# Two passes of a down-projection piece held back and issued behind the next block's first gate/up product

## The chip, the cores and the metric

The kernel runs on one core of a Trainium2 chip. The metric is the device time of one execution in microseconds (us). TensorE (PE in the profile) multiplies, with its weight loads shown as PEld; VectorE is DVE, ScalarE is ACT, GpSimd is POOL, and SyncE (SP) issues most DMAs.

## The reference

Two layers of a decoder trunk over 512 tokens of width 1024. Each layer has a mixer of three kinds of heads, a gated MLP, and a per-layer embedding. The part in which the change lies is the MLP and the projection of the embedding:

```python
def conv_gated_mlp(h, w_gate, w_up, conv_w, conv_b, w_down):
    g = h @ w_gate                      # 512 x 1024 by 1024 x 4096
    gp = jnp.pad(g, ((0, 0), (CONV_WIDTH - 1, 0), (0, 0)))
    conv = conv_b + gp[:, 0:S] * conv_w[0]
    for j in range(1, CONV_WIDTH):
        conv = conv + gp[:, j:j + S] * conv_w[j]
    act = jax.nn.gelu(conv, approximate=True) * (h @ w_up)
    return act @ w_down                 # 512 x 4096 by 4096 x 1024
...
h = rmsnorm(x, ffn_pre_g[i])
x = x + rmsnorm(conv_gated_mlp(h, ...), ffn_post_g[i])
gate = jax.nn.sigmoid(rmsnorm(x, ple_pre_g[i]) @ w_ple_gate[i])
e = p[i] @ w_ple_proj[i]                # 512 x 256 by 256 x 1024
x = x + rmsnorm(e * gate, ple_post_g[i])
```

Everything is float32.

## The kernel before

**Products in three passes.** A float32 product is made of two rounded halves of each operand, high and low (`split`: ACT writes the high half, DVE the low half). `mm3` issues three passes for each 128 rows of contraction: high by high, high by low, low by high. A pass is one MATMUL with its own weight load of 128 by 128.

**The MLP in 32 blocks.** Block `b` makes 128 of the 4096 gate and up columns, for all 512 tokens. `gate_up(b)` does this with seven products in place of eight (a Strassen-like scheme): the tokens are two halves of 256, the contraction two halves of 512. Each product is 4 x 3 = 12 passes of 256 columns. Its names, in the order in which they are recorded, with the names that the profile shows:

| product | written to | operands in the profile |
|---|---|---|
| b11 | `be`, bank `beta` | `beta<-hb,wg` |
| b21 | `al`, bank `ag` | `ag<-hb,wg` |
| h6 | `be` | `beta<-hh,wsa` |
| d | `ga`, bank `ag` | `ag<-hd,wsa` |
| h7 | `be` | `beta<-hh,wsb` |
| b22 | `ga` | `ag<-hb,wsb` |
| h4 | `be` | `beta<-hh,wu` |

`be` keeps accumulating over four products. Between them ACT copies it out (`gs<-beta` behind b11 and behind h6), DVE reads it (`us<-beta,us` behind h7), and the next product into `be` waits for that read. So h6 waits for ACT, h7 for ACT, and h4 for DVE's `us`. In the same way d waits for DVE's `gs<-ag,gs`, and b22 for ACT's `us<-ag`.

**The down projection in pieces.** Every four blocks give 512 columns of the activation (`act`, two blocks to a tile). They are multiplied with their part of `w_down` one group of four later: eight pieces `down(q, c, u)`, one for each 128 tokens `c` and each half of the output. A piece is 4 x 3 = 12 passes of 512 columns into a PSUM bank `dn` (`dn<-thl,act`), and DVE adds the bank to an accumulator (`facc<-dn,facc`; ACT copies it for the first group). Blocks 4 to 31 of a layer issue such pieces behind their seven products, mostly two each, so 24 passes; the last group's eight pieces stand behind the blocks. `embed` makes the product of the embedding ahead of block 0 (`eps<-ehl,pT`: 8 pieces of 6 passes, each copied out by ACT and stored by a DMA from SP's queue).

**What sets the order.** The code records every operation in a `Plan`. `Plan.issue` then walks the recorded operations with estimated costs (`cost`), takes on each engine the earliest recorded one that is ready, and so fills PE's expected waits with passes recorded later. What comes out is issued through one line (L396), so the profile's rows are told apart by tiles. The built program differs a little from the plan's order, because the layer underneath also moves a few PE instructions; the rows shown below are those of the built program. Large tiles come from two sets of slots (`SETS`), and `pick` chooses the set.

Of the kernel before, what the change touches and what calls it, by code (L numbers as in the profile page):

```python
# [32 lines left out]
ALU = mybir.AluOpType  # L33
# [5 lines left out]
NCH = 4  # L39
# [10 lines left out]
class Plan:  # L50
# [18 lines left out]
    def __init__(self):  # L69
        self.ops = []  # L70
        self.table = {}
        self.tiles = {}
        self.real = {}
        self.kind = {}
        self.place = {}
        self.scratch = bacc.Bacc("TRN2", target_bir_lowering=False, num_devices=1)

    def pool(self, pool, psum=False):

# [62 lines left out]
    def record(self, engine, fn, method, args, kw):  # L142
        i = len(self.ops)
        outs, ins = [], []
        first = True
        for k, v in [(None, v) for v in args] + list(kw.items()):
            if not isinstance(v, bass.AP):
                continue
            is_out = k in ("out", "accum_out") or (k is None and first)
            if k is None:  # L150
                first = False
            (outs if is_out else ins).append(v)
        deps, used = set(), []
        for aps, write in ((ins, False), (outs, True)):
            for ap in aps:
                name = ap.tensor.name
                if name not in self.tiles or self.tiles[name][0] == "junk":
                    continue
                t = self.tiles[name]
                used.append(name)  # L160
                r = (0, P, [(0, 512)]) if t[3] else self.region(ap)
                for j, w, q in t[2]:
                    if (write or w) and j != i and j not in deps and self.overlap(r, q):
                        deps.add(j)
                t[2].append((i, write, r))
        if engine == "PE":
            t = self.tiles[outs[0].tensor.name]
            if len(t) > 6:
                deps.add(t[6])
            t[6:] = [i]  # L170
        self.ops.append((engine, fn, args, kw, deps, used, self.cost(engine, method, outs, ins, args, kw)))

    def cost(self, engine, method, outs, ins, args, kw):

        def size(ap):
            n = 1
            for d in ap.shape[1:]:
                n *= d
            return n

        if "dma" in method:
            return (820 if engine == "POOL" else 525) if outs[0].shape[0] > 2 else 700, 4.0 * size(outs[0]) * outs[0].shape[0]
        n = size(ins[0] if method == "tensor_reduce" else outs[0])
        psum = any(self.tiles[v.tensor.name][3] for v in ins + outs)
        scalars = [kw.get(k) for k in ("scalar", "scalar1", "scalar2", "bias", "scale")]
        pointers = sum(isinstance(v, bass.AP) for v in scalars)
        if engine == "PE":
            if method == "transpose":
                return 108, 0, n
            dt, rows = kw["lhsT"].dtype, kw["lhsT"].shape[0] / P  # L190
            if dt == F32R:
                return 0.4416 * n + 6, 0, n * rows
            half = 0.5 if kw["lhsT"].shape[0] == 64 or kw["lhsT"].shape[-1] == 64 else 1
            return half * max(222, n * 4 / 2.4 + 4) if dt == F32 else max(56, n / 2.4), 0, (2 if dt == F32 else 1) * n * rows
        if engine == "ACT":
            func = ([v for v in args if isinstance(v, AF)] + [None])[0]
            self.table[len(self.ops)] = func if func in self.TABLES else None
            pointers += method == "mul" and isinstance(args[2], bass.AP)
            return (50 if psum else 97) + n / 1.196 + 93 * pointers + 93 * ("accum_out" in kw), 0
        if engine == "POOL":  # L200
            if n > 64:
                return 155 + n * (2.09 if method == "tensor_tensor" else 0.86), 0
            if kw.get("op") == ALU.pow:
                return 300 + 165 * n, 0
            return 160 if pointers == 0 else 200 + 64 * pointers, 0
        rate = 0.96
        if method == "reciprocal":
            rate /= 8
        elif method in ("tensor_copy", "tensor_scalar") and not psum:
            rate *= 2  # L210
        return 68 + 62 * bool(pointers) + n / rate, 0

    def issue(self):
        ops = self.ops
        n = len(ops)
# [10 lines left out]
        first, last, slots, live = {}, {}, {}, {}  # L226
# [18 lines left out]
        done = [False] * n  # L245
        front = 0
# [23 lines left out]
        def pick(t):  # L270

            if self.kind[t] is not None:
                c, s = self.kind[t], first[t]
                return c if unused[c] and (s <= front or inside[c][front:s].max() < self.SETS[c]) else None
            room = [(self.SETS[c] - inside[c][front:last[t] + 1].max(), c) for c in self.SETS if unused[c]]
            spare, c = max(room, default=(0, None))
            return c if spare > 0 else None

        def take(i, now):
            o = ops[i]  # L280
# [70 lines left out]
        while len(order) < n:  # L351
            progress = False
            for e in names:
                while waiting[e] and waiting[e][0][0] <= now:
                    _, pr, i = heapq.heappop(waiting[e])
                    heapq.heappush(ready[e], (pr, i))
                if ready[e] and free[e] <= now:
                    _, i = heapq.heappop(ready[e])
# [108 lines left out]
def body(ctx, tc, a, out):  # L467
# [259 lines left out]
    def mm3(ps, lhs, rhs, first, last, skip=False):  # L727
        for i, (h, r) in enumerate(((0, 0), (0, 1), (1, 0))):
            T.matmul(ps, lhsT=lhs(h), rhs=rhs(r), start=first and i == 0, stop=last and i == 2, skip_group_check=skip)
# [317 lines left out]
    def ffn(l, hs, emb, x, new, g, nxt):  # L1047
# [11 lines left out]
        def product(ps, w, n, first, last):  # L1059
            for k in range(4):  # L1060
                ks = slice(k * P, k * P + P)
                mm3(ps, lambda i: w[i][:, ks], lambda i: h[n][:, i, k, :], first and k == 0, last and k == 3, True)

        def gate_up(b):
            raw = b8("graw", (2048,))
            load(raw, a["w_gu"][l, b].rearrange("p s n -> p (s n)"))
            u2, g1, g2, u1 = (raw[:, i * 512:i * 512 + 512] for i in range(4))
# [19 lines left out]
            def part(t, i):  # L1087
                return [t[:, j, i * 512:i * 512 + 512] for j in range(2)]
            product(be, part(wg, 0), "b11", True, False)
            A.copy(gs[:, t1], be)  # L1090
            product(al, part(wg, 1), "b21", True, True)
            V.tensor_tensor(out=gs[:, t1], in0=al, in1=gs[:, t1], op=ALU.add)
# [19 lines left out]
            t = acts[b // 2]  # L1112
            split(t[:, 0, b % 2, :], t[:, 1, b % 2, :], cv)

        def down(q, c, u):

            ps = bank("dn")
            ts = slice(c * P, c * P + P)
            for j in range(4):
                t = acts[2 * q + j // 2]  # L1120
                mm3(ps, lambda i: t[:, i, j % 2, ts], lambda i: u(i, j), j == 0, j == 3)
            return ps

        def wd(q, hf):
            return tm_units(a["w_dn"][l, q, hf], 512, 4)

        embed(l, *emb)
        for b in range(32):
            gate_up(b)
            q, i = divmod(b, 4)  # L1130
            if not q:
                continue
            i0, i1 = ((0, 2, 4, 6, 8) if q < 7 else (0, 1, 3, 5, 8))[i:i + 2]
            for hf, c in [divmod(j, 4) for j in range(i0, i1)]:
                if c == 0:
                    u = wd(q - 1, hf)
                ps = down(q - 1, c, u)
                if q == 1 and hf == 0 and c % 2 == 0:
                    facc.append(b8("facc", (2, D)))
                fr = facc[c // 2][:, c % 2, hf * 512:hf * 512 + 512]  # L1140
                if q == 1:
                    A.copy(fr, ps)
                else:
                    V.tensor_tensor(out=fr, in0=ps, in1=fr, op=ALU.add)

        us = [wd(7, hf) for hf in range(2)]
        for c in range(NCH):
# [1 line left out]
        for c in range(NCH):  # L1149
            fr = facc[c // 2][:, c % 2, :]  # L1150
            parts = []
            for hf in range(2):
                ps = down(7, c, us[hf])
                cs = slice(hf * 512, hf * 512 + 512)
                V.tensor_tensor(out=fr[:, cs], in0=ps, in1=fr[:, cs], op=ALU.add)
                parts.append(post_part(fr[:, cs], g[:, 0, cs], fr[:, cs]))
            post_chunk(x[c], parts, fr, stored=new[:, c, :])
            nxt(c, x[c])
# [25 lines left out]
    def embed(l, pT, us):  # L1184

        e = [b8("e", (2, D)) for _ in range(2)]
        for hf, u in enumerate(us):
            cs = slice(hf * 512, hf * 512 + 512)
            for c in range(NCH):
                ps = bank("eps")  # L1190
                ts = slice(c * P, c * P + P)
                for k in range(2):
                    mm3(ps, lambda i: pT[:, i, k, ts], lambda i: u[:, i, k, :], k == 0, k == 1)
                A.copy(e[c // 2][:, c % 2, cs], ps)
                SY.dma_start(out=ed[l][:, c, cs], in_=e[c // 2][:, c % 2, cs])

    ov = out[0].rearrange("(c p) d -> p c d", p=P)

# [92 lines left out]
```

## Time and profile before

| | us |
|---|---|
| time before, median of 3 runs (1637.95 to 1641.28) | 1638.48 |
| the profiled execution's own time | 1644.15 |
| its span, first to last instruction | 1642.3 |
| PE busy in the span | 1598.1 (97%) |
| DVE, ACT busy in the span | 1240.5, 840.4 |

The profiled execution is 5.7 us longer than the median, 1.9 us of its own time lie outside its span. A row of the timeline gives the start of a run of equal instructions and its stretch; matmuls are pipelined, so what a run takes is the difference between its start and that of the next run. In the groups and the windows, busy time is summed over overlapping instructions.

### The profile page before, as it was taken

To read this page: it belongs to the slowest core of one execution; us is meant where nothing else is said; L and a number is where in the kernel's file an instruction comes from. 1 tells how busy PE (TensorE), PEld (TensorE's weight loads), DVE (VectorE), ACT (ScalarE), POOL (GpSimd) and SP (SyncE) were. 2 spreads that over 40 slices of the span, in tenths; PEclk is the share of its full clock that TensorE was granted. 3 is DMA by queue.
4 is the path that set the end of the run, shared out by engine and by line. 5 is a ranking of instruction groups with operands and counts; after the bars stand their busy time and mean duration, and the time that the engine had idled before them with its cause. 6 is when DMAs were issued, how large, how long until landed. Compare 5 with 4: busy or idle time off the path is not lost.

```text
span 1642.3 us, 25129 instructions
## 1 busy us (share of the span) xinstructions
PE 1598.1 (97%) x10034; PEld 1411.3 (86%) x10034; DVE 1240.5 (76%) x1949; ACT 840.4 (51%) x1378; POOL 90.5 (6%) x157
## 2 busy tenths in 40 slices
PE   5999999999999999999999999989999999999998
PEld 4887687999999999998878776879999999999987
DVE  6456758987888888786764568599788788788784
ACT  5435626765554554554562346276555555555453
POOL 1100012000000000001220000110000000000022
PEclk9999999999999999999999999999999999999999
DMA  7313316323324323236552133172334233233441
GB/s 281 104 38 129 105 64 216 118 79 128 103 78 129 100 81 129 97 103 256 193 172 82 65 103 116 53 253 82 104 103 129 78 104 129 77 103 129 173 161 65
DMA packets 63422, 197.48 MB, mean 120 GB/s; under 512 B 7349, under 2 KB 15165, under 8 KB 63305
## 3 DMA queue, kind: packets, MB, share of 16 engines
q1 hardware_dynamic: 63016, 195.28, 35.1%
q8 instruction: 79, 1.29, 0.3%
q10 hardware_dynamic: 288, 0.59, 0.1%
q14 instruction: 39, 0.31, 0.1%
HBM read 178.52 MB, written 17.33 MB: 119 GB/s over the span
## 4 chain that ended last, share of the span: by engine, by line
PE 71%; DVE 5%; ACT 3%; DMA 3%; issue 1%; POOL 1%; SPq 0%; POOLq 0%; DVEq 0%; ACTq 0%
PE beta L396 20%; PE dn L396 20%; PE ag L396 15%; PE ps L396 7%; PE fps L396 2%; PE rps L396 2%; PE wo L396 1%; DVE x L396 1%; PE gps L396 1%; DMA traw<-in_w_dn_dram 1%; ACT junk L396 1%; DMA e<-e 1%; PE hps L396 1%; PE ops L396 0%; ACT thl L396 0%
## 5 line engine op out<-in xcount | busy, mean ns | idle before, releaser
L396 PE MATMUL dn<-thl,act 128*128 128x512 f32 x1536 | 368.0, 390 | 0.0
L396 PEld LDWEIGHTS dn<-thl,act 128*128 128x128 f32 x1536 | 282.7, 188 | 54.0
L396 PE MATMUL ps<-thl,hT 128*128 128x512 f32 (+3 forms) x984 | 206.3, 369 | 0.0
L396 PEld LDWEIGHTS ps<-thl,hT 128*128 128x128 f32 x984 | 178.2, 190 | 21.9
L396 DVE TENSOR_TENSOR thl<-traw,thl 128x1024 fp32r<-128x1024 f32 (+2 forms) x120 | 141.3, 1187 | 37.0 <-ACT thl L396 36.2
L396 ACT CAST thl<-traw 128x1024 fp32r<-128x1024 f32 (+2 forms) x120 | 121.0, 1019 | 44.9 <-PE fps L396 11.1
L396 PE MATMUL beta<-hb,wg 128*128 128x256 f32 x768 | 105.8, 283 | 5.6 <-DVE wg L396 5.6
L396 PEld LDWEIGHTS beta<-hb,wg 128*128 128x128 f32 x768 | 101.5, 191 | 10.3 <-DVE wg L396 6.0
L396 ACT COPY gs<-beta 128x256 f32<-128x256 f32 x128 | 47.6, 372 | 112.1 <-PE beta L396 112.0
L396 PE MATMUL ag<-hb,wg 128*128 128x256 f32 x768 | 103.2, 283 | 0.0
L396 PE MATMUL beta<-hh,wsa 128*128 128x256 f32 x768 | 101.8, 282 | 1.2 <-ACT gs L396 0.9
L396 PE MATMUL beta<-hh,wsb 128*128 128x256 f32 x768 | 101.7, 281 | 0.2
L396 PE MATMUL beta<-hh,wu 128*128 128x256 f32 x768 | 101.7, 282 | 0.2
L396 DVE TENSOR_TENSOR wsa<-ws,wsa 128x1024 fp32r<-128x1024 f32 x64 | 78.2, 1221 | 31.2 <-ACT wsa L396 25.7
L396 PEld LDWEIGHTS beta<-hh,wu 128*128 128x128 f32 x768 | 93.9, 188 | 9.0 <-DVE us L396 7.6
L396 PE MATMUL ag<-hd,wsa 128*128 128x256 f32 x768 | 100.8, 281 | 0.7 <-DVE gs L396 0.7
L396 PE MATMUL ag<-hb,wsb 128*128 128x256 f32 x768 | 100.7, 280 | 0.0
L396 PEld LDWEIGHTS beta<-hh,wsa 128*128 128x128 f32 x768 | 95.4, 190 | 2.1 <-ACT gs L396 1.4
L396 PEld LDWEIGHTS ag<-hb,wg 128*128 128x128 f32 x768 | 96.6, 191 | 0.0
L396 DVE SCALAR_TENSOR_TENSOR cv<-gs,cw,cv 128x511 f32<-128x511 f32 (+1 forms) x128 | 95.5, 746 | 1.4 <-ACT cv L396 0.3
L396 PEld LDWEIGHTS beta<-hh,wsb 128*128 128x128 f32 x768 | 94.6, 189 | 1.5 <-ACT gs L396 1.3
L396 PEld LDWEIGHTS ag<-hd,wsa 128*128 128x128 f32 x768 | 94.7, 189 | 1.3 <-DVE gs L396 1.1
(194 smaller groups left out, 2711.8 us busy)
## 6 DMA issues: line engine op xcount, KB each, us to landing
graw<-in_w_gu_dram SPq DMA_DIRECT2D x128, 512.0 KB
traw<-in_w_dn_dram SPq DMA_DIRECT2D x64, 512.0 KB
x<-x SPq DMA_DIRECT2D x40, 512.0 KB
fraw<-in_w_fm_dram SPq DMA_DIRECT2D x30, 512.0 KB
traw<-in_w_wo_dram SPq DMA_DIRECT2D x16, 512.0 KB
traw<-in_w_pg_dram SPq DMA_DIRECT2D x16, 512.0 KB
traw<-in_w_uv_dram SPq DMA_DIRECT2D x8, 512.0 KB
e<-e SPq DMA_DIRECT2D x16, 256.0 KB
```

Of the source, the lines that this page charges most:

```text
L396: o[1](*[self.map(v) for v in o[2]], **{k: self.map(v) for k, v in o[3].items()})
```

## The change

The last piece that a block issues (for block 0 the last piece of `embed`) is cut: its last two passes are handed to the next block as `rest()` and recorded between b11 and b21. A new `fence` makes the plan's next PE operation depend on the newest one, on both sides of the two passes. Blocks 0 and 5 to 31 of each layer get such a rest, 28 a layer. With the two passes moves what reads the bank: the `facc` add, and for `embed` ACT's copy and the store of the last 128 tokens' second half. The plan's cost for these passes goes from `0.4416 * n + 6` to `0.4427 * n` ns for n columns, and `pick` may take a full set's free slot for a tile whose first use has come up.

```diff
+    def fence(self):
+
+        self.fenced = True
...
         if engine == "PE":
+            if self.fenced:
+                deps.add(self.newest)
+            self.newest, self.fenced = i, False
             t = self.tiles[outs[0].tensor.name]
...
             if dt == F32R:
-                return 0.4416 * n + 6, 0, n * rows
+                return 0.4427 * n, 0, n * rows
...
-            return c if spare > 0 else None
+            return c if spare > 0 or first[t] <= front else None
...
-        def gate_up(b):
+        def gate_up(b, rest):
...
             product(be, part(wg, 0), "b11", True, False)
+            if rest:
+                plan.fence()
+                rest()
+                plan.fence()
             A.copy(gs[:, t1], be)
             product(al, part(wg, 1), "b21", True, True)
...
-        def down(q, c, u):
+        def down(q, c, u, done):
...
             for j in range(4):
                 t = acts[2 * q + j // 2]
-                mm3(ps, lambda i: t[:, i, j % 2, ts], lambda i: u(i, j), j == 0, j == 3)
-            return ps
+                for i, (h, r) in enumerate(((0, 0), (0, 1), (1, 0))):
+                    if j < 3 or not i:
+                        T.matmul(ps, lhsT=t[:, h, j % 2, ts], rhs=u(r, j), start=j == 0 and i == 0, stop=False)
+
+            def rest():
+                T.matmul(ps, lhsT=t[:, 0, 1, ts], rhs=u(1, 3), start=False, stop=False)
+                T.matmul(ps, lhsT=t[:, 1, 1, ts], rhs=u(0, 3), start=False, stop=True)
+                done(ps)
+            return rest
...
-        embed(l, *emb)
+        rest = embed(l, *emb)
         for b in range(32):
-            gate_up(b)
+            gate_up(b, rest)
+            rest = None
...
-                ps = down(q - 1, c, u)
...
+                def add(ps, q=q, fr=facc[c // 2][:, c % 2, hf * 512:hf * 512 + 512]):
+                    if q == 1:
+                        A.copy(fr, ps)
+                    else:
+                        V.tensor_tensor(out=fr, in0=ps, in1=fr, op=ALU.add)
+                if rest:
+                    rest()
+                rest = down(q - 1, c, u, add)
+        rest()
```

In `embed`, the last piece likewise issues four of its six passes and returns the other two, with the copy and the store, as the rest. The pieces of the last group run their rest at once.

The first place is block 13 of the first layer on PE, from its first product to the passes that follow its seventh. Before:

```order
L396 MATMUL beta<-hb_2154,wg 128x256 x12
L396 MATMUL ag<-hb_2169,wg 128x256 x12
L396 MATMUL beta<-hh_2239,wsa 128x256 x12
L396 MATMUL ag<-hd,wsa 128x256 x12
L396 MATMUL beta<-hh_2248,wsb 128x256 x12
L396 MATMUL ag<-hb_2228,wsb 128x256 x12
L396 MATMUL dn<-thl,act 128x512
L396 MATMUL beta<-hh_2266,wu 128x256 x12
L396 MATMUL dn<-thl,act 128x512 x23
```

And now:

```order
L404 MATMUL beta<-hb_2154,wg 128x256 x12
L404 MATMUL dn<-thl,act 128x512 x2
L404 MATMUL ag<-hb_2169,wg 128x256 x12
L404 MATMUL beta<-hh_2240,wsa 128x256 x12
L404 MATMUL ag<-hd,wsa 128x256 x12
L404 MATMUL beta<-hh_2249,wsb 128x256 x12
L404 MATMUL dn<-thl,act 128x512
L404 MATMUL ag<-hb_2234,wsb 128x256 x12
L404 MATMUL dn<-thl,act 128x512
L404 MATMUL beta<-hh_2267,wu 128x256 x12
L404 MATMUL dn<-thl,act 128x512 x20
```

Two passes of the preceding block's piece now stand between b11 and b21, and one pass each ahead of b22 and of h4, where before one stood ahead of h4 alone.

The second place is the next block on PE, block 14. Before, its rows were those of block 13 with two passes ahead of h4 in place of one. Now, from b21 to the passes behind h4:

```order
L404 MATMUL ag<-hb_2169,wg 128x256 x12
L404 MATMUL dn<-thl,act 128x512 x4
L404 MATMUL beta<-hh_2240,wsa 128x256 x2
L404 MATMUL dn<-thl,act 128x512 x3
L404 MATMUL ag<-hd,wsa 128x256 x2
L404 MATMUL dn<-thl,act 128x512
L404 MATMUL beta<-hh_2240,wsa 128x256 x10
L404 MATMUL ag<-hd,wsa 128x256 x10
L404 MATMUL beta<-hh_2249,wsb 128x256 x12
L404 MATMUL ag<-hb_2234,wsb 128x256 x12
L404 MATMUL dn<-thl,act 128x512
L404 MATMUL beta<-hh_2267,wu 128x256 x12
```

Here h6 and d are cut after their first two passes, the ones that need only the high half of the weights `wsa`, and eight down passes stand where the low half, which DVE writes, is waited for. Of four blocks that follow each other in the middle of a layer, one has this shape (block 14), one that of block 13, one a single pass ahead of h7 (block 15), and one nothing but the two passes behind b11 (block 12).

The third place is the start of the MLP on PE. Before:

```order
L396 MATMUL eps<-ehl,pT 128x512 x20
L396 MATMUL beta<-hb_2154,wg 128x256 x2
L396 MATMUL ag<-hb_2169,wg 128x256 x2
L396 MATMUL beta<-hb_2154,wg 128x256 x10
L396 MATMUL ag<-hb_2169,wg 128x256 x10
```

And now:

```order
L404 MATMUL eps<-ehl,pT 128x512 x16
L404 MATMUL beta<-hb_2154,wg 128x256 x2
L404 MATMUL eps<-ehl,pT 128x512 x2
L404 MATMUL ag<-hb_2169,wg 128x256 x2
L404 MATMUL beta<-hb_2154,wg 128x256 x2
L404 MATMUL ag<-hb_2169,wg 128x256 x2
L404 MATMUL beta<-hb_2154,wg 128x256 x10
```

The two held passes of `embed` stand behind the first two passes of block 0, and four passes of block 1 have come ahead of the third pass of b11. Elsewhere the new costs move single passes in the mixers, and ACT loads its function tables 17 times in place of 15, both more in the first layer's mixer (the sine and the GELU alternate once more).

More of the change, by code (lines that the diff above doesn't have):

```diff
@@ L73, in __init__ @@
         self.real = {}
+        self.fenced = False
         self.kind = {}
@@ L1136, in ffn @@
                     u = wd(q - 1, hf)
-                ps = down(q - 1, c, u)
                 if q == 1 and hf == 0 and c % 2 == 0:
                     facc.append(b8("facc", (2, D)))
[L1140 to L1144, printed above, removed]
+                def add(ps, q=q, fr=facc[c // 2][:, c % 2, hf * 512:hf * 512 + 512]):
[7 more added lines that the diff above has]
+        rest()
         us = [wd(7, hf) for hf in range(2)]
@@ L1152, in ffn @@
             for hf in range(2):
-                ps = down(7, c, us[hf])
                 cs = slice(hf * 512, hf * 512 + 512)
-                V.tensor_tensor(out=fr[:, cs], in0=ps, in1=fr[:, cs], op=ALU.add)
+                down(7, c, us[hf], lambda ps: V.tensor_tensor(out=fr[:, cs], in0=ps, in1=fr[:, cs], op=ALU.add))()
                 parts.append(post_part(fr[:, cs], g[:, 0, cs], fr[:, cs]))
@@ L1191, in embed, with some @@
                 ts = slice(c * P, c * P + P)
[L1192 to L1195, printed above, removed]
+                passes = [(k, h, r) for k in range(2) for h, r in ((0, 0), (0, 1), (1, 0))]
+                def some(passes, ps=ps, u=u, c=c, cs=cs, ts=ts):
+                    for k, h, r in passes:
+                        T.matmul(ps, lhsT=pT[:, h, k, ts], rhs=u[:, r, k, :], start=(k, h, r) == (0, 0, 0), stop=(k, h) == (1, 1))
+                    if passes[-1][:2] == (1, 1):
+                        A.copy(e[c // 2][:, c % 2, cs], ps)
+                        SY.dma_start(out=ed[l][:, c, cs], in_=e[c // 2][:, c % 2, cs])
+                if hf and c == NCH - 1:
+                    some(passes[:4])
+                    return lambda: some(passes[4:])
+                some(passes)
     ov = out[0].rearrange("(c p) d -> p c d", p=P)
```

## The prediction

> **What bounds the kernel now.** I read the page first: busy time and the chain that ended last.
>
> ```profile
> PE 1598.1 (97%) x10034; PEld 1411.3 (86%) x10034; DVE 1240.5 (76%) x1949; ACT 840.4 (51%) x1378; POOL 90.5 (6%) x157
> PE beta L396 20%; PE dn L396 20%; PE ag L396 15%; PE ps L396 7%; PE fps L396 2%; PE rps L396 2%; PE wo L396 1%; DVE x L396 1%; PE gps L396 1%; DMA traw<-in_w_dn_dram 1%; ACT junk L396 1%; DMA e<-e 1%; PE hps L396 1%; PE ops L396 0%; ACT thl L396 0%
> ```
>
> TensorE is the bound, and the MLP (`beta`, `ag`, `dn`) is 55% of the chain. So I went to four blocks in the middle of a layer, in windows and then row by row.
>
> ```profile
> core 0: us, PE busy (x) PEld busy (x) DVE busy (x) ACT busy (x) POOL busy (x), PEclk, DMA share, GB/s
> 432.52:494.32 61.80, 61.80 (x434) 57.48 (x433) 51.33 (x68) 31.89 (x49) 0.00 (x0) 1.00 0.32 104
> ```
>
> Four blocks take 61.80 us with PE never idle, the clock at 1.00, and DVE at 51.33 (83%). A shorter time there can only come from passes that go faster, or from waits that hide inside PE's rows. The timeline of a block shows both:
>
> ```profile
> 432.52 1.58 PE L396 MATMUL beta<-hb,wg 128*128 128x256 f32 x12
> 433.93 1.58 PE L396 MATMUL ag<-hb,wg 128*128 128x256 f32 x12
> ...
> 441.00 0.39 PE L396 MATMUL dn<-thl,act 128*128 128x512 f32 x1
> ...
> 441.34 1.45 PEld L396 LDWEIGHTS beta<-hh,wu 128*128 128x128 f32 x12 [0.27 <-DVE us L396]
> 441.34 1.64 PE L396 MATMUL beta<-hh,wu 128*128 128x256 f32 x12
> ...
> 442.82 5.40 PE L396 MATMUL dn<-thl,act 128*128 128x512 f32 x23
> ...
> 448.06 0.28 PE L396 MATMUL beta<-hb,wg 128*128 128x256 f32 x1
> ```
>
> The first product's 12 passes take 433.93 - 432.52 = 1.41 us (118 ns a pass); all six up to 441.00 take 8.48, again 1.41 each. Before h4 the weight load waits 0.27 us for DVE's `us`. The 23 passes of 512 columns take 5.24 us, 0.228 each. Now the same products at another place:
>
> ```profile
> 726.26 1.58 PE L396 MATMUL beta<-hh,wsa 128*128 128x256 f32 x12
> 727.68 0.63 PE L396 MATMUL dn<-thl,act 128*128 128x512 f32 x2
> 728.14 1.53 PE L396 MATMUL ag<-hd,wsa 128*128 128x256 f32 x12
> 729.51 1.52 PE L396 MATMUL beta<-hh,wsb 128*128 128x256 f32 x12
> 730.87 1.52 PE L396 MATMUL ag<-hb,wsb 128*128 128x256 f32 x12
> 732.23 0.63 PE L396 MATMUL dn<-thl,act 128*128 128x512 f32 x2
> ```
>
> Two down passes happened to be put between h6 and d. Ahead of them h6 takes 1.42; behind them d takes 1.37, h7 1.36 and b22 1.36: 113 ns a pass on the same tiles, with no wait. So passes of 256 columns have two levels, and two passes of 512 between products bring the fast one, which then lasts. The other instances agree:
>
> ```profile
> 425.67 0.63 PE L396 MATMUL dn<-thl,act 128*128 128x512 f32 x2
> 426.14 1.53 PE L396 MATMUL beta<-hh,wu 128*128 128x256 f32 x12
> 427.50 5.17 PE L396 MATMUL dn<-thl,act 128*128 128x512 f32 x22
> ...
> 456.54 1.58 PE L396 MATMUL beta<-hh,wu 128*128 128x256 f32 x12
> 457.95 0.63 PE L396 MATMUL dn<-thl,act 128*128 128x512 f32 x2
> ```
>
> Behind two passes h4 takes 1.36; with none ahead of it, 1.41. Behind the 22 to 24 passes that end a block the level is slow again (the 432.52 row follows the 427.50 run). Transfers are not the cause, as two stretches show, one inside a slow product and one inside the fast h4 at 441.34:
>
> ```profile
> 435.34:436.70 1.36, 1.36 (x14) 1.36 (x13) 1.09 (x2) 0.00 (x0) 0.00 (x0) 1.00 0.00 0
> 441.60:442.80 1.20, 1.20 (x12) 1.20 (x12) 0.55 (x2) 1.20 (x2) 0.00 (x0) 1.00 1.00 410
> ```
>
> The slow one has no DMA (the last two columns), the fast one all of it. The reader is to see that the level depends on what ran just before, not on tile, product, clock or transfers.
>
> **The change, part by part.** It puts exactly such a pair behind b11 in 54 blocks (5 to 31 of both layers), 13.5 groups of four. I price a group.
>
> *The level.* b11 stays slow. The other six products go from 6 x 1.413 = 8.48 to 1.37 + 5 x 1.36 = 8.17: 0.31 a block, 1.24 a group. Three of four h4 are fast already (behind a pair, or behind a wait as at 441.34), which takes off 0.15, and stray fast products some 0.05 more: **-1.04**.
>
> *The passes themselves.* Nothing is added or removed; the same 96 passes run. A pair by itself takes 728.14 - 727.68 = 0.46 to 0.47, against 2 x 0.228 in a long run: +0.01 each. With the other pieces into which the new order cuts the down passes (some seven more a group, up to 0.02 each), less those of the old order: **+0.10**.
>
> *The waits.* What stands queued behind a waiting weight load is all of PE. The waits row counts them:
>
> ```profile
> PEld beta L396 <- DVE us L396: 7.6, 27, 0.4
> PEld beta L396 <- DVE wg L396: 6.0, 2, 3.1
> ```
>
> 27 waits for `us` in 54 blocks, two a group. One costs (441.34 - 441.00 - 0.228) + (1.48 - 1.36) = 0.23, so 0.46 a group now. In the new order every place with one pass ahead of a product is a place where the product wasn't yet ready for the planner: b22 and h4 in block 13, the rest of h6 and h4 in block 14, h7 in block 15, five a group. Faster products also give DVE and ACT 0.05 us less for each answer. Between none (-0.46) and all five (1.15, +0.69) I take three, since the single passes ahead of h4 are what waits now and those ahead of other products mostly don't: **+0.23**.
>
> *Falling back.* A single pass may also undo the fast level:
>
> ```profile
> 344.41 0.40 PE L396 MATMUL dn<-thl,act 128*128 128x512 f32 x1
> 344.64 1.58 PE L396 MATMUL ag<-hd,wsa 128*128 128x256 f32 x12
> 346.06 1.58 PE L396 MATMUL beta<-hh,wsb 128*128 128x256 f32 x12
> ...
> 373.69 0.39 PE L396 MATMUL dn<-thl,act 128*128 128x512 f32 x1
> 373.92 1.53 PE L396 MATMUL beta<-hh,wsa 128*128 128x256 f32 x12
> 375.28 1.52 PE L396 MATMUL ag<-hd,wsa 128*128 128x256 f32 x12
> ```
>
> One pass without a wait left the level slow at 344 (d 1.42) and made it fast at 373 (h6 1.36); from the fast level no row shows it. If it always fell back, block 15 would lose 3 products x 0.05, block 13 two, block 14 nearly five: 0.52 a group. Where PE waits it comes back fast (442.82 - 441.34 is 0.12 over the fast product, the rest of the wait), so only the places that don't wait can lose: between 0 and 0.52 I take half of two in five, **+0.12**.
>
> Sum: -1.04 + 0.10 + 0.23 + 0.12 = -0.59 a group, x 13.5 = -8.0 us.
>
> *The start of the MLP.* Both layers wait for DVE's `wg`, 6.0 us in two waits (second row above). Four passes of block 1 now run ahead of that wait, 4 x 0.118 = 0.47 a layer: **-0.9**. The two held passes of `embed` stood ahead of the wait before and still do. Their copy and their store come a few passes later; the store is on SP's queue among the weight loads, and whoever reads it comes after the 32 blocks, so I price it at 0 (lower end 0, upper end the 0.6 us of one copy).
>
> *What costs nothing.* The `facc` add comes some 1.9 us later (b11 and the pair), on a DVE with 10 us free in 61.80; bank, `act` and `thl` are held that long. If DVE's cover goes, the next split of weights is late (third rival). Two more table loads stand on ACT in the first layer:
>
> ```profile
> L396 ACT ACT_TABLE_LOAD x2 | 2.6, 1283 | 0.0
> ```
>
> 2.6 us on an engine that is busy 51% of the span; between 0 and 2.6 I take 0, since PE, the bound, has other passes to run there. Other moves in the mixers I put at 0 within 2 us either way. Total -8.9: from the profiled execution's own 1644.15 to 1635.3, and from the median, 5.7 lower, 1638.48 to 1629.6; I say 1629.5.
>
> [...]
>
> **The rivals.** (A) *Nearly the whole gain.* The new order's single passes fill every wait and keep the level: waits 0, no falling back. -1.04 + 0.10 - 0.46 = -1.40 a group, -18.9 - 0.9: 1618.7. For it: the pair ahead of h4 (426.14) has no wait. Against: 27 waits behind single passes now.
>
> (B) *The level isn't moved.* The pair brings the fast level where it stood by chance, behind h6 and b22, but not behind b11, and 118 ns stays. Only +0.10 x 13.5 - 0.9 is left: 1639, no change. For it: no row has a pair behind b11, whose passes follow a long run of 512 columns. Against: the h4 at 426.14 and the d at 728.14 follow different products and tiles, and both are fast.
>
> (C) *Slower: PE waits for the split of `wsa` in block 14's shape.* PE there has only eight down passes until DVE's low half of `wsa`. DVE's instructions of that kind are long:
>
> ```profile
> L396 DVE TENSOR_TENSOR wsa<-ws,wsa 128x1024 fp32r<-128x1024 f32 x64 | 78.2, 1221 | 31.2 <-ACT wsa L396 25.7
> ```
>
> One such instruction in the way adds 1.22 a group: -0.59 + 1.22 = +0.63, x 13.5 = +8.5 - 0.9: 1646. It decides from 0.66 us a group on ((8.0 + 0.9) / 13.5). For it: h6 is cut there at just that dependency. Against: DVE has 17% free, and before no row of PE in these blocks waits for `wsa`.
>
> **How the numbers follow.** Forecast 0.72, with its own range 1623 to 1637 (two waits fewer or two more, falling back never or always where nothing waits, 2 us of the mixers); A 0.12; B 0.09; C 0.07. About 0.2% (3.3 us) is what a measurement of this kernel can tell from no change. Faster: nearly all of the forecast (0.70) and A, 0.82. Same: B and the forecast's upper edge, 0.11. Slower: C, 0.07. The range takes in A's end and the lower half of C: 1619 to 1641.
>
> **What would show it.** Right: in the timeline behind b11 a `dn` run of 2 and then products of 1.36; four blocks in 60.6 to 61.6; waits for `us` still some tens; h7 behind block 15's single pass shows whether the level falls back. Wrong: products of 1.41 behind the pair (B), a PE wait for `wsa` in every fourth block (C), or almost no waits (A).

## The result and the profile after

The changed kernel takes **1643.41 us** (1640.55 to 1647.23) beside 1638.48 before: ratio 1.0028, interval 1.0018 to 1.0037. It is slower by 5 us, where 9 us less were forecast. Its profiled execution took 1643.52 us, span 1641.7.

The page's first line, and two successive groups of four blocks by windows:

```profile
PE 1594.9 (97%) x10034; PEld 1403.1 (85%) x10034; DVE 1235.7 (75%) x1949; ACT 838.4 (51%) x1380; POOL 103.4 (6%) x157
```
```profile
443.51:505.55 62.04, 61.66 (x433) 56.78 (x432) 50.67 (x69) 31.27 (x48) 0.00 (x0) 1.00 0.31 102
505.55:567.20 61.65, 61.61 (x434) 56.86 (x433) 51.06 (x69) 31.47 (x48) 0.00 (x0) 1.00 0.31 103
```

PE is now idle for up to 0.38 us in a group, where before no idle showed, and a group is about as long as it was (61.80). The first block of the first group (block 12), in the timeline:

```profile
443.51 1.58 PE L404 MATMUL beta<-hb,wg 128*128 128x256 f32 x12
444.93 0.63 PE L404 MATMUL dn<-thl,act 128*128 128x512 f32 x2
445.39 1.53 PE L404 MATMUL ag<-hb,wg 128*128 128x256 f32 x12
446.76 1.52 PE L404 MATMUL beta<-hh,wsa 128*128 128x256 f32 x12
448.12 1.52 PE L404 MATMUL ag<-hd,wsa 128*128 128x256 f32 x12
449.98 1.64 PE L404 MATMUL beta<-hh,wsb 128*128 128x256 f32 x12 [0.34 <-ACT gs L404]
451.47 1.52 PE L404 MATMUL ag<-hb,wsb 128*128 128x256 f32 x12
452.83 1.52 PE L404 MATMUL beta<-hh,wu 128*128 128x256 f32 x12
454.19 5.17 PE L404 MATMUL dn<-thl,act 128*128 128x512 f32 x22
```

The level is moved as predicted: b21 takes 446.76 - 445.39 = 1.37, h6 1.36, b22 and h4 1.36. But from d to h7 it is 449.98 - 448.12 = 1.86, because h7 waits for ACT's `gs`: one wait has cost 0.50, twice what the five faster products gained (0.05 each). The waits of PE's weight loads in the blocks:

```profile
PEld beta L404 <- DVE us L404: 6.3, 23, 0.4
PEld beta L404 <- DVE wg L404: 5.5, 2, 2.9
PEld beta L404 <- ACT gs L404: 4.5, 9, 1.3
PEld ag L404 <- DVE gs L404: 2.8, 8, 0.3
```

So two questions stand: why the level brings so little in the blocks, and where the 5 us more come from.

### The profile page after: what moved, and what is told of

Its sections match the earlier page's. It is cut to its first block, busy times and chain, and to the rows that moved or that the text cites. A ratio compares the mean times of both kernels' runs of the same rounds, so it can differ in the third digit from the quotient of the medians.

```text
span 1641.7 us, 25133 instructions
## 1 busy us (share of the span) xinstructions
PE 1594.9 (97%) x10034; PEld 1403.1 (85%) x10034; DVE 1235.7 (75%) x1949; ACT 838.4 (51%) x1380; POOL 103.4 (6%) x157
## 5 line engine op out<-in xcount | busy, mean ns | idle before, releaser
L404 PE MATMUL dn<-thl,act 128*128 128x512 f32 x1536 | 386.7, 391 | 0.0
L404 PEld LDWEIGHTS dn<-thl,act 128*128 128x128 f32 x1536 | 277.8, 188 | 47.4
L404 ACT CAST wg<-graw 128x1024 fp32r<-128x1024 f32 x64 | 67.2, 1051 | 60.9 <-DMA graw<-in_w_gu_dram 36.4
```

Of the source, the lines that this page charges most:

```text
L404: o[1](*[self.map(v) for v in o[2]], **{k: self.map(v) for k, v in o[3].items()})
```

## The experiments

**Before once more (b_again).** 

> The kernel before, once more, for a second trace of it. The first one belongs to an execution 5.7 us over the median. If the trace of after is short of its gain because before's first trace was long, the second trace is about 1636 to 1637 us long and shows at which stage the first one lost the 5 us; four blocks in the middle of a layer stay at 61.8 us.

Measured: 1635.32 us. The first trace of before had lost 2.0 us in the first layer's output product, 2.0 at block 1, 3.2 at the border of the layers (where the first MLP ends and the second layer's `fps` begin) and 1.6 later. Stages and blocks are compared with this second trace from here on. Against it, after is 8.2 us longer: first layer to the end of its MLP -1.3, **border of the layers +9.7**, second layer to the end of its MLP -1.2, rest +1.0. The border itself:

```profile
825.22 0.36 PEld L396 LDWEIGHTS rbps<-k_ident,rs 128*128 128x128 f32 x2
825.55 3.26 PEld L396 LDWEIGHTS ps<-thl,hT 128*128 128x128 f32 x15
829.29 0.42 PEld L396 LDWEIGHTS hps<-k_ident,h 128*128 128x128 f32 x4 [0.48 <-issue]
```

and in after:

```profile
819.31 5.80 PEld L404 LDWEIGHTS ps<-thl,hT 128*128 128x128 f32 x26
829.55 0.72 PEld L404 LDWEIGHTS hps<-k_ident,h 128*128 128x128 f32 x4 [4.44 <-ACT junk L404]
```

Before has 15 passes of the gate product ahead of the transposes `hps`; after has none there, and PE's weight loads stand 4.44 us. Around and behind that wait the granted clock is 0.51 (828.30 to 835.30 us), where this trace of before stays at 1.00. That is a move outside the MLP, which the prediction had put at 0 within 2 us.

**One part at a time (b_move, a_oldcost, b_both).** Three kernels: before's order on all engines with only the two passes and their add moved; after with the old cost; before with the new cost (and `pick`'s edit, which was not run alone).

```diff
+        for held, add, b11 in self.moves:      # b_move: behind the plan's loop
+            ... # held to behind the last op of b11, add to where it is ready
-                return 0.4427 * n, 0, n * rows         # a_oldcost
+                return 0.4416 * n + 6, 0, n * rows
-                return 0.4416 * n + 6, 0, n * rows     # b_both
+                return 0.4427 * n, 0, n * rows
```

> Before's own order on all engines, with only the two passes (and the facc add behind them) moved behind b11 in blocks 5 to 31 of both layers; no new costs, embed not cut. Theory 1 (the passes give their gain, the new cost of a pass and the order that follows from it take it away): 1638.5 - 8 = 1630, four blocks at 61.2 us. Theory 2 (faster products only make PE wait longer for ACT and DVE, whatever the order): four blocks at 61.6 or more, 1636 to 1639.

> After, with the old cost 0.4416 * n + 6: the held passes, the fences and the cut of embed, planned anew with the old cost. Theory 1: near the kernel with the passes moved alone, 1630 give or take 3, four blocks at 61.2. Theory 2: 1638 to 1643, like after, four blocks at 61.6. A third theory (any new planning of the mixers and of the first blocks comes out some us to either side, by chance): four blocks at 61.2, and the loss or gain in the stages outside the blocks.

> Before with the new cost 0.4427 * n alone (and the edit of pick, without which this cost leaves the plan without an operation to issue); nothing held back. Theory 1: it loses what after lost, 1638.5 + 13 = 1651, with more PE waits for ACT and DVE in the blocks. Theory 2: the cost does little, 1637 to 1641. The third theory: blocks at 61.8 as before, the other stages changed by up to 5 us in all.

Measured: moved alone 1635.81 (0.9984, 0.9976 to 0.9992); held with the old cost 1636.84 (0.9991, 0.9982 to 1.0001); new cost alone 1644.03 (1.0031, 1.0019 to 1.0043). So both halves of the result show: the cost loses 5 to 7 us, with or without the held passes, and the held passes bring 1 to 3 where 8 were expected. Moved alone, a group takes 61.6 us, as the second theory had it. Held with the old cost, the time fits neither of the first two theories (1630, and 1638 to 1643): a group takes 61.5 us and the border is 4.9 us longer, nearest to the third. The new cost alone lies between its first two (1651, and 1637 to 1641). The border's wait for `junk` also stands with the passes held and the old cost (4.45 us), and not with the new cost alone: it comes with the held passes and their new plan, not with the cost. The same block before and then with the passes moved; for each h6 on PE, three rows of DVE, and h4's weight load:

```profile
461.95 1.58 PE L396 MATMUL beta<-hh,wsa 128*128 128x256 f32 x12
...
465.75 0.69 DVE L396 TENSOR_TENSOR ws<-ws,graw 128x512 f32<-128x512 f32 x1
466.36 1.22 DVE L396 TENSOR_TENSOR wsa<-ws,wsa 128x1024 fp32r<-128x1024 f32 x1
467.50 0.42 DVE L396 SCALAR_TENSOR_TENSOR us<-beta,us 128x256 f32<-128x256 f32 x1
...
467.96 1.00 PEld L396 LDWEIGHTS beta<-hh,wu 128*128 128x128 f32 x8 [0.29 <-DVE us L396]
```
```profile
461.89 1.52 PE L407 MATMUL beta<-hh,wsa 128*128 128x256 f32 x12
...
465.70 0.69 DVE L407 TENSOR_TENSOR ws<-ws,graw 128x512 f32<-128x512 f32 x1
466.31 1.22 DVE L407 TENSOR_TENSOR wsa<-ws,wsa 128x1024 fp32r<-128x1024 f32 x1
467.44 0.42 DVE L407 SCALAR_TENSOR_TENSOR us<-beta,us 128x256 f32<-128x256 f32 x1
...
467.91 1.00 PEld L407 LDWEIGHTS beta<-hh,wu 128*128 128x128 f32 x8 [0.50 <-DVE us L407]
```

From h6 to h4 it is 6.01 us before and 6.02 with faster products. h6, d, h7 and b22 are each 0.05 us shorter, and the wait for `us` is 0.21 longer. DVE sets the stretch: it goes without a gap from `ws` into a split of `wsa` of 1.22 us, and `us`, which h4 needs, stands behind that split. Summed over blocks 5 to 31, PE's gaps ahead of products that wait (start to start, less a pass's usual time) grew from about 3.6 us (26 places) to 9.3 (43), and those at h4 from 3.2 to 6.6. The second pass of a product that has waited starts late as well (222 and 224 ns behind the first in these two h4, where 118 is usual); with it the waits grew from 6.6 to 14.2 us.

**The split kept behind `us` (bm_pin_wsa, b_pin_wsa).** In the plan, `us` stands ahead of the split; the layer underneath puts the split first. This edit keeps the low half of `wsa` behind everything that the plan put ahead of it on DVE:

```diff
+            if i in self.pinned:          # the low half of wsa
+                tc.keep_in_program_order(ins)
```

> The two passes moved in before's order, and DVE's low half of wsa (1.22 us) kept behind what the plan put ahead of it, so that DVE's us of the block stands ahead of it in 24 of the blocks where h4 waits. Theory A (PE's faster products end up in the wait of h4 for us, because DVE has just begun a split of 1.22 us): the 24 waits at h4 (6.6 us) mostly go, 1630 to 1632. Theory B (DVE as a whole is the bound in these stretches, so a split that comes 0.5 us later is waited for elsewhere): 1634 to 1637, with waits at d, h7, b22 or at the next block's b21.

> The same edit of DVE's order in before, nothing held back. Theory A: its 24 waits at h4 hold 3.2 us, of which h4's fast level behind a wait gave 24 x 0.05 back, so 1638 - 2 = 1636; the pair's own gain then comes in full on top of it in the kernel with both. Theory B: no change, 1638.

Measured: with the passes moved **1628.69** (0.9939, 0.9927 to 0.9951); without them 1635.18 (0.9971, 0.9961 to 0.9981). Theory A held, a little better than written, and theory B fell. The same block with the passes moved and the split kept:

```profile
465.04 0.69 DVE L408 TENSOR_TENSOR ws<-ws,graw 128x512 f32<-128x512 f32 x1
465.65 0.42 DVE L408 SCALAR_TENSOR_TENSOR us<-beta,us 128x256 f32<-128x256 f32 x1
465.98 1.22 DVE L408 TENSOR_TENSOR wsa<-ws,wsa 128x1024 fp32r<-128x1024 f32 x1
...
466.91 1.54 PE L408 MATMUL beta<-hh,wu 128*128 128x256 f32 x12
```

`us` is done before b22 ends, and h4 follows its single pass without a wait; the gaps at h4 fell from 6.6 to 0.1 us. The held passes are now worth 6.5 us (1635.18 - 1628.69; 5.2 by the ratios), two to three times what they were worth with the split in the way.

**How many passes lift the level (bm1_pin, bm4_pin, bm3_pin).** As bm_pin_wsa, with one, four or three passes held back (`held = tuple(range(n - k, n))`).

> As the kernel with the two passes moved and wsa's split kept in its place (1628.7), but with one pass held back in place of two. If any pass of 512 columns between products lifts the level, the time and the products' 1.36 us stay: 1629. If it takes two, all six products stand at 1.41 us and the time is that of the kernel with the split alone kept in its place: 1635.

> The same with four passes held back. After's trace has a run of four behind a slow product that was followed by slow ones (at 353 us), and runs of three that were followed by fast ones. If four leave the level slow as there: 1635, products of 1.41 us; if not, 1629 and 1.36.

> Three passes held back, everything else as in the kernels with one (1627.5, fast) and four (1633.4, slow). Products of 1.36 us behind the three if the level is lifted by fewer than four passes of 512 columns, as after's single row with three has it; 1.41 and some 1633 if one and two are all that lifts it.

Measured: one 1627.49 (0.9940, 0.9926 to 0.9953), three 1627.67 in a single execution, four 1633.43 (0.9973, 0.9961 to 0.9984). Behind one pass, then behind four:

```profile
442.74 0.39 PE L408 MATMUL dn<-thl,act 128*128 128x512 f32 x1
442.97 1.53 PE L408 MATMUL ag<-hb,wg 128*128 128x256 f32 x12
444.34 0.39 PE L408 MATMUL beta<-hh,wsa 128*128 128x256 f32 x2
```
```profile
429.69 1.09 PE L408 MATMUL dn<-thl,act 128*128 128x512 f32 x4
430.62 1.58 PE L408 MATMUL ag<-hb,wg 128*128 128x256 f32 x12
432.04 1.58 PE L408 MATMUL beta<-hh,wsa 128*128 128x256 f32 x12
```

b21 takes 1.37 behind one pass and 1.42 behind four. Here one to three passes lift the level and four leave it; four cost as much as no pass at all (the ratio without held passes is 0.9971).

**Where the new cost loses (a_mlpcost, a_outcost, ao_pin_wsa, a_pin_wsa).** The cost split by place, and the split of `wsa` kept in after with the old and the new cost.

```diff
-                return 0.4427 * n, 0, n * rows
+                return 0.4427 * n if self.inner else 0.4416 * n + 6, 0, n * rows       # a_mlpcost; a_outcost: not self.inner
```

> After, with the new cost only for what is recorded from embed to the end of the 32 blocks, the old cost elsewhere. If the new cost hurts by its order of the blocks and of embed, this is as slow as after, 1642 to 1644; if by the order of the mixers, the embedding's gate and the borders of the stages, it is near the kernel with the old cost, 1636 to 1638. The stages of the traces say half and half, 1640.

> The complement: the old cost from embed to the end of the blocks, the new cost elsewhere. 1636 to 1638 if the cost hurts in the blocks, 1642 to 1644 if it hurts outside them, 1640 if half and half.

> After with the old cost, and wsa's split kept where the plan has it. Theory A again: the waits at h4 (5.2 us) go, 1636.8 - 6 = 1631. It stays 2 to 3 us behind the kernel with before's order (1628.7), because its plan leaves PE 4.4 us without work where the first layer's embedding gate meets the second layer's mixer, and half a clock for some passes behind it.

> After as it is (new cost, cut of embed), with wsa's split kept where the plan has it. If its loss against the kernel with the old cost (6.6 us) lies in the blocks, in the waits of h4, b22 and h7, this one gains more than the 6.7 us that the same edit gave there: 1634 or below. If it lies in the other stages, it gains 4 to 6 (after has 3.8 us of waits at h4) and stays 7 us behind the old cost's 1630: 1638 to 1639.

Measured: new cost inside 1638.35 (0.9998, 0.9988 to 1.0007), outside 1637.67 (0.9991, 0.9981 to 1.0001), so 1.5 and 0.8 us over the old cost's 1636.84 (1.1 and 0.0 by the ratios), not 6.6: the parts don't add up, and by place of the cost the question has no answer. With the split kept, the old cost gives 1630.17 (0.9960, 0.9947 to 0.9974), about as expected, a gain of 6.7 (5.1 by the ratios), and the new cost 1641.93 (1.0016, 1.0006 to 1.0027), a gain of 1.5, less than either case expected: there the gaps at h4 went too (3.8 to 0.5 us), but those at b22 rose from 0.8 to 6.5. In the ten long ones b22 waits for ACT's copy `us`, 0.36 us long, which stands behind a cast of weights of 1.05 us; eight of these casts had themselves waited 0.9 to 1.8 us for the DMA of `w_dn`. With the new cost alone the gaps at b22 are 6.7 us, of the same kind; that is about what that kernel loses in all, though other terms moved too. The 4.4 us at the border stayed in both.

**All in the plan's own order (bm_pin_three, a_pin_three, b_pin_three, ao_pin_three, bc_pin_three).** Every instruction of PE, ACT and DVE stays behind its engine's previous one, so that the layer underneath moves nothing on them:

```diff
+            if o[0] in ("DVE", "ACT", "PE"):
+                tc.keep_in_program_order(ins)
```

> The two passes moved, and all of PE, ACT and DVE issued in the plan's own order, so that nothing is moved behind the plan. If the moves behind the plan are bad in general, faster than 1628.7, down to 1625 (the waits left at d and h7, 2.8 us, stand behind splits of w_down); if only the split of wsa mattered, 1628 to 1632.

> After with all of PE, ACT and DVE issued in the plan's own order. If the new cost is bad because the layer behind the plan moves instructions away from what it planned, this comes near the same kernel with the old cost and before's plan, 1629 to 1632. If the plan itself is worse (its estimates run ahead of ACT and DVE), it stays above 1634.

> Before with all of PE, ACT and DVE issued in the plan's own order: nothing held back, old cost. If the plan's order by itself is what is worth the time, this is near 1621 too. If the held passes and the new cost only pay in the plan's own order, this is 1633 to 1637, with products at 1.41 us and few waits, since the old cost, 0.119 us a pass, fits the slow level.

> The held passes with the old cost, in the plan's own order. The plan counts 1.43 us for a product that takes 1.36, so PE comes early and waits remain: 1626 to 1629, some 4 us of waits in the blocks.

> The new cost alone, nothing held back, in the plan's own order. The plan counts 1.36 us for products that mostly take 1.41, so PE comes late and hardly waits; the gain is that of pairs that the plan puts between products by itself: 1630 to 1636. If the cost were bad in itself: 1640 and more.

Measured, medians in us:

| | neither | passes held | new cost | both |
|---|---|---|---|---|
| as built | 1638.0 to 1639.5 | 1636.84 | 1644.03 | 1643.41 |
| in the plan's order | 1636.86 | 1623.82 | 1628.25 | **1620.81** |
| ratio to before, in the plan's order | 0.9983 (0.9974 to 0.9992) | 0.9906 (0.9893 to 0.9920) | 0.9929 (0.9916 to 0.9942) | 0.9888 (0.9870 to 0.9905) |

The passes moved in before's plan give 1628.99 (0.9949, 0.9936 to 0.9961), no better than with the split alone kept: there only the split mattered. After, issued as it was planned, is the fastest kernel of all, 22.6 us under itself as built and 1.1% under before. Four of its blocks, one block's products, and all PE waits in `beta` and `ag`:

```profile
424.87:485.48 60.61, 60.61 (x434) 56.73 (x433) 50.52 (x68) 31.35 (x49) 0.00 (x0) 1.00 0.29 105
```
```profile
429.48 1.52 PE L404 MATMUL ag<-hd,wsa 128*128 128x256 f32 x12
430.84 0.40 PE L404 MATMUL dn<-thl,act 128*128 128x512 f32 x1
431.07 1.53 PE L404 MATMUL beta<-hh,wsb 128*128 128x256 f32 x12
432.44 1.52 PE L404 MATMUL ag<-hb,wsb 128*128 128x256 f32 x12
```
```profile
PEld beta L404 <- DVE wg L404: 5.7, 2, 2.9
PEld beta L404 <- DVE wsa L404: 0.7, 2, 0.3
```

The waits for `us` and `gs` are gone; summed over blocks 5 to 31 the gaps are at most 0.25 us, where after as built has about 8. The group takes 60.6 us. Against after as built, blocks 6 to 30 gain 13.7 us (both layers), blocks 0 to 5 gain 5.1, the border of the layers 5.1; the 4.4 us ahead of `hps` are gone.

This kernel and after as built have one plan, so their traces show what the layer underneath does. By the names of the tiles, at least 501 of 1949 instructions of DVE, 317 of 1380 of ACT and 93 of 10034 of PE stand in another order in after as built: not a few of PE alone. The wait of 0.50 us in the block shown above is such a move. ACT there, and then in the same block in the plan's order:

```profile
448.61 1.05 ACT L404 CAST wg<-graw 128x1024 fp32r<-128x1024 f32 x1 [3.12 <-DMA graw<-in_w_gu_dram]
449.57 0.36 ACT L404 COPY gs<-beta 128x256 f32<-128x256 f32 x1
```
```profile
444.76 0.37 ACT L404 COPY gs<-beta 128x256 f32<-128x256 f32 x1 [2.82 <-PE beta L404]
446.12 0.37 ACT L404 COPY us<-ag 128x256 f32<-128x256 f32 x1 [0.99 <-PE ag L404]
446.91 1.05 ACT L404 CAST wg<-graw 128x1024 fp32r<-128x1024 f32 x1
```

As built, the cast of a later block's gate weights stands ahead of `gs`, and ACT has waited 3.12 us for that cast's DMA; in the plan's order both copies that PE needs come first. All eight waits over 0.25 us that ACT ends at h7 and b22 in after have a long instruction (0.63 to 1.06 us) just ahead of the short copy.

Of the expectations for the table, the one with neither held (1633 to 1637). The other three came out better than written: the cost alone 1628.25 against 1630 to 1636, both 1620.8 against 1629 to 1632, and the held passes with the old cost 1623.8 against 1626 to 1629, with 1.6 us of gaps in place of 4.

## Why the prediction was wrong, by its own steps

- **The level, -1.04 a group (-14.0 us): right in kind, a little large.** Counted by their start-to-start gaps, products' passes under 116 ns went from 1284 of 5376 to 3831 with the passes moved, and 2547 x 4.45 ns = 11.3 us; in after to 3367, 9.3 us. In the plan's own order the held passes are worth 1636.86 - 1623.82 = 13.0 us. Rival B, that the level isn't moved, is out, though its time (1639) was nearer to the result than the forecast.
- **The passes themselves, +0.10 a group: about right.** The pair takes 0.470 in place of 0.454: 0.8 us in 54 blocks; single passes between products add 0.4 in after, and the long runs are unchanged.
- **Waits, +0.23 a group (3.1 us): mis-sized, and the step that failed in the blocks.** With the passes moved alone the gaps grew by 5.7 us, in after by 4.4. Priced as the prediction did, with the late pass behind a wait, they grew by 7.7 and 6.2 us, 0.57 and 0.46 a group. The prediction counted places and priced each as today's wait; it took the products' saving as 0.05 us for each answer. But in the block shown ACT's cast of `wg` starts as b21 ends, DVE's `wg` behind it, and from there DVE runs without a gap to `us` (463.18 to 467.44, and 463.23 to 467.50 before), so four products' savings come back at one wait, 0.21 at this h4. Its own upper bound for this term, +0.69 a group, would have held it. In after, -9.3 for the level, +6.2 for the waits and +1.2 for the passes leave -1.9 in the blocks; the two stretches with the MLPs measure -2.5.
- **Falling back, +0.12 a group behind single passes: seldom, and not the main cause.** A single pass mostly lifts the level by itself (1.37 behind one). In after, 4 of 39 single passes without a wait let the fast level fall. Where one product follows another with nothing between, it fell at 6 of 20 waits, so "where PE waits it comes back fast" does not hold there, while it held at all 12 waits behind a single pass; the last section has the counts over all traces. What the falls cost in all was not measured apart.
- **The start of the MLP, -0.9: not there.** From block 0 to block 5 it is 60.03 and 59.72 us in after's two layers, 59.99 and 59.46 in before's second trace; the wait for `wg` is 5.5 us in two against 4.9.
- **The new cost and the mixers' moves, 0 within 2 us: the largest error.** The cost is worth +6.0 us alone and +6.6 with the held passes, as built. The border of the layers alone is 9.7 us longer in after: 4.9 of it stands with the old cost too, the rest came with the new one. The prediction gave no row for the 0. In the plan's own order the cost is even a gain of 3.0 to 8.6 us; of the 8.6, some 5.1 are 1145 more fast passes, since its plan puts more down passes between products by itself, and 3.4 are blocks 0 to 5. What the prediction did not see is the layer underneath: it was taken to move a few PE instructions, and it moves DVE's and ACT's too, long casts ahead of the short copies that PE waits for, so a better plan came out as a worse program.
- **The rivals.** A's time, 1618.7, with every wait filled, is near what after comes to in the plan's order (1620.8), in part by luck: blocks 0 to 5 give 4.6 us of that and the border takes 4.7 back. C named the right instruction, DVE's split of `wsa`, for the wrong reason: PE does not wait for it, it waits for `us` behind it. C's sum, 1646, was near the result by other terms: no row of PE in after's blocks waits for `wsa`.

Open is what in the layer underneath makes its moves. Which instruction carries a loss was seen for the split of `wsa`, for ACT's casts and for the border, and only the split was put back by itself. The two more table loads and `pick`'s edit were not tried alone.

## What to carry to other kernels

Before a new order is priced, see whether the order on the chip is the planned one, on every engine and not only on the bound: here the same change is 5 us slower or 18 us faster by that alone. When the bound engine's instructions get faster, look for a gapless chain on another engine between two of its waits: here four products' 0.05 us each came back as 0.21 us of wait behind DVE's chain to `us`. Find the short answer that stands behind a long instruction there, and let it go first. Measure one part with everything else held in place (the move alone, in the old order) before you explain a mixture.

## What the runs showed of the hardware that was not expected

**The level depends on the run of passes in between, and not by a simple limit.** Over all traces of this case, runs of 512-column passes that follow a slow product and end without a wait lifted the passes of 256 columns from 118 to 113 ns in 124 of 134 cases for one pass, 680 of 682 for two, all 104 for three, none of 68 for four, all 4 for five (h6 takes 1.38 behind the five at 354.51 in the kernel with the new cost alone), and never for eight or more. Why is open, and the number of passes was not told apart from the time that they take. Where a product follows a fast one with nothing between, the level stays in 2998 of 3014 cases without a wait, and falls in 72 of 190 with one over 25 ns. The kernel with three held passes shows such a fall, where h7 comes late behind d (446.10 to 447.73 is 1.63):

```profile
446.10 1.52 PE L408 MATMUL ag<-hd,wsa 128*128 128x256 f32 x12
447.73 1.68 PE L408 MATMUL beta<-hh,wsb 128*128 128x256 f32 x12
449.24 1.58 PE L408 MATMUL ag<-hb,wsb 128*128 128x256 f32 x12
450.66 1.58 PE L408 MATMUL beta<-hh,wu 128*128 128x256 f32 x12
```

**The same wait with and without a slower clock.** At the border of the layers PE's weight loads wait 2.34 us for `rs`, in the first trace of before and in the kernel with the passes moved alone. Behind it the windows show, for before and then for the other:

```profile
836.70:840.20 3.50, 3.50 (x12) 2.72 (x11) 2.20 (x3) 1.21 (x3) 1.80 (x2) 0.54 0.26 97
```
```profile
831.00:834.50 3.50, 3.50 (x19) 2.90 (x18) 2.20 (x3) 1.21 (x3) 1.72 (x2) 1.00 0.30 112
```

The granted clock is 0.54 in one and 1.00 in the other: passes of 512 columns start 427 ns apart in the first and some 230 in the second, so 12 instructions of PE run in place of 19 in the same time. In the first trace of before, while PE has work, the half clock begins at 205.51, 280.60 and 836.97 us, which are 22 and 163 times 3.413 us apart, and lasts 3.41 or 6.83 us. In the 3.41 us ahead of each PE was busy for 1.42, 1.48 and 1.30 us. Cut into such stretches from 25 us to the end of PE's work, the trace has no other with less than 1.68, and no half clock begins behind any other. PE's idle time of 1.97 us ahead of 1016.19 and that of 2.76 us ahead of 1090.98 each lie across a border of two stretches (1.68 us or more of PE's work in each), and no half clock follows. In after it begins at 282.24, 828.37 and 1091.20 us, behind 1.44, 0.57 and 0.99 us of work in 3.41; every other stretch there at full clock, from 25 us on and up to the one in which PE's work ends, has 2.3 or more. That the pause in the kernel with the passes moved alone lay across a border too (at 828.85) is the author's estimate, from that trace's own stretches; what sets the clock beyond these figures was not shown. The clock also goes with the spread between executions: of the 27 of before taken beside the kernel with the split kept, the six with a mean granted clock of 0.995 have a median of 1641.5 us, the eight with 0.998 one of 1637.9.
